# Feed-forward input products of a decoder step: plain blocks replaced by seven products on halves

## The chip, the core and the metric

The kernel runs on one core of one Trainium2 chip. The metric is device time in microseconds for one execution. A core has TensorE (matmuls, with weight loads in a row of their own), VectorE, ScalarE, GpSimd and a queue engine, SyncE, each with an instruction stream of its own, and 16 DMA engines.

## What is computed

One step of a two-layer decoder trunk on 1024 prompt tokens and 8 sample tokens (T = 1032), width 1024: a gated linear recurrence, a feed-forward, a latent attention, a feed-forward. Of the reference, what matters here:

```python
def rmsnorm(x, gain):
    y = xf * lax.rsqrt(jnp.mean(xf * xf, axis=-1, keepdims=True) + EPS)
    return y * gain

def swiglu(h, w_in, w_out):
    g, u = jnp.split(h @ w_in, 2, axis=-1)      # w_in 1024 x 5632
    return (jax.nn.silu(g) * u) @ w_out         # w_out 2816 x 1024

x = x + rmsnorm(mix, g[1])
x = x + rmsnorm(swiglu(rmsnorm(x, g[2]), w_ffn_in[l], w_ffn_out[l]), g[3])
```

## The kernel before, in words

Tokens lie along the free dimension in NS = 3 spans of W = 344 columns; the width lies in KC = 8 chunks of 128 partitions. Every large product is done in three passes: each operand is split into a high and a low fp32r part, and `mm3` (L172) multiplies high by high, high by low and low by high into one PSUM bank (lines L177, L178, L179), each matmul with its own 128 x 128 weight load. `xproduct` (L184) runs `mm3` over the eight chunks of one span: 24 matmuls of 344 columns. `split` (L127) makes a high part on ScalarE (L129) and a low part on VectorE (L130). `weight` (L132) loads 512 KB of weights on SyncE's queue, casts the high part on ScalarE (L151) and subtracts the low part on GpSimd (L155, two pieces of 512).

The four stages follow each other: `hgrn`, `ffn0`, `mla`, `ffn1`. The feed-forward (`ffn`, L533) goes over NF = 22 blocks of 128 hidden columns. For each block and span, `inp` makes g and u by two `xproduct`s, multiplies both by the reciprocal root `r` of the token's mean square (L552, L556 on VectorE: x itself is not normalised), applies silu (L553, ScalarE), multiplies (L557, GpSimd) and splits into `gh`, `gl`. The output products of the block before run between: `out_chunk` for 3 spans x 8 output chunks, 3 matmuls each (72 a block), evacuated by an addition into `acc` on VectorE (L582). The last LAST = 3 blocks are multiplied in `outf` inside the final norm.

`finish` (L296) ends every stage but the last. Per span, `products` makes the eight output chunks and `norm` runs a span behind: reciprocal root of the sum of squares (`rstd`, L192, L198), multiplication into `acc` (L324), residual addition (L325), `put_x` (L213: high and low part of x, L221 and L222, not normalised), squares (L241), and at the end the second root `r`. For the last span that root is left to the feed-forward: the squares are added up into two tiles `ss` (L336), and `r` is made when `inp` first needs it. Four `xproduct`s of the next stage on spans 0 and 1 are run ahead in `finish`.

The engines run in their own order; a tile framework adds the waits and orders the instructions of an engine by program order and due times. Buffers of a pool are reused in turn, which makes a later writer wait for the last reader.

## Time and profile before

| | before |
|---|---|
| median of 3 runs | 2925.95 us (2925.64 to 2926.82) |
| profiled execution | 2927.77 us, its span 2926.0 us |
| TensorE matmul, weight load busy | 2790.2 us (95%), 2623.6 us (90%) |
| VectorE, ScalarE, GpSimd busy | 1718.8 (59%), 1129.5 (39%), 999.3 us (34%) |
| mean DMA rate | 83 GB/s |
| mean granted TensorE clock | 0.977 |

The page comes from one profiled execution. Matmuls are pipelined: their busy times overlap, and the start-to-start time of neighbours tells how fast they go. Weight loads have records of their own (PEld) and overlap the matmuls. A wait is put down to what released it last.

### The profile page before, as it was taken

What the parts mean: (1) busy time and instruction counts of PE and PEld (TensorE: products, weight loads), DVE (VectorE), ACT (ScalarE), POOL (GpSimd) and SP (SyncE); (2) the same over time, 40 slices, a digit from 0 to 9 for tenths busy, and PEclk for the clock granted to TensorE, in tenths of its full rate; (3) what the DMA queues carried; (4) which work ended last, traced back from release to release, by engine and by line L of the source; (5) the groups of instructions that cost most, each with busy time, mean ns of one, the idle gap of its engine ahead of it and who ended that gap; (6) DMA issues with size and microseconds to landing.
All of it is one profiled execution on the core that took longest, in us unless ns stands there. A gap on an engine that the chain in (4) does not pass through costs nothing.

```text
span 2926.0 us, 54566 instructions
## 1 busy us (share of the span) xinstructions
PE 2790.2 (95%) x22360; PEld 2623.6 (90%) x22360; DVE 1718.8 (59%) x3298; ACT 1129.5 (39%) x2422; POOL 999.3 (34%) x912
## 2 busy tenths in 40 slices
PE   7998988889999999999999999979999999999998
PEld 7988888878899999999978899846889999999998
DVE  7888888863444444444358888794363444444435
ACT  7666666655511111111255766523453111111112
POOL 3555555552432233332332111242153332223320
PEclk9999999989999999999999999989999999999999
DMA  5122222152311111111132112486431111111112
GB/s 184 54 67 67 67 67 65 60 191 99 117 48 50 44 44 51 46 49 51 37 100 83 46 48 69 169 346 223 133 107 51 47 48 51 44 44 49 46 61 92
DMA packets 230970, 242.51 MB, mean 83 GB/s; under 512 B 19074, under 2 KB 211120, under 8 KB 224704
## 3 DMA queue, kind: packets, MB, share of 16 engines
q1 hardware_dynamic: 205456, 170.14, 19.0%
q0 software_dynamic: 7456, 43.00, 4.0%
q10 hardware_dynamic: 17808, 25.89, 2.5%
q8 instruction: 176, 2.88, 0.4%
q14 instruction: 74, 0.61, 0.1%
HBM read 194.87 MB, written 44.12 MB: 82 GB/s over the span
## 4 chain that ended last, share of the span: by engine, by line
PE 83%; DVE 9%; ACT 4%; issue 2%; DMA 1%; POOL 1%; SPq 0%; DVEq 0%; ACTq 0%; POOLq 0%
PE ps L177 24%; PE ps L178 24%; PE ps L179 23%; PE ps L252 2%; DVE E L873 1%; DVE turned L1458 1%; PE ps L1385 1%; PE ps L1458 1%; DVE X L877 1%; PE ps L903 1%; PE ps L940 1%; ACT E L875 1%; DVE X L1008 1%; PE ps L198 1%; DVE oy L1010 1%
## 5 line engine op out<-in xcount | busy, mean ns | idle before, releaser
L177 PE MATMUL ps<-xh,w 128*128 128x344 f32 x3360 | 1103.8, 329 | 1.9 <-ACT xh L221 1.9
L178 PE MATMUL ps<-xl,w 128*128 128x344 f32 x3360 | 1083.5, 323 | 1.6 <-DVE xl L222 1.6
L179 PE MATMUL ps<-xh,w 128*128 128x344 f32 x3360 | 1078.7, 322 | 0.0
L155 POOL TENSOR_TENSOR w<-raw,w 128x512 fp32r<-128x512 f32 (+1 forms) x360 | 466.3, 1316 | 809.5 <-ACT w L151 803.0
L177 PEld LDWEIGHTS ps<-xh,w 128*128 128x128 f32 x3360 | 638.6, 190 | 24.7 <-issue 12.1
L178 PEld LDWEIGHTS ps<-xl,w 128*128 128x128 f32 x3360 | 638.5, 190 | 15.3 <-issue 8.3
L179 PEld LDWEIGHTS ps<-xh,w 128*128 128x128 f32 x3360 | 637.5, 190 | 5.7 <-issue 5.6
L582 DVE TENSOR_TENSOR acc<-ps,acc 128x344 f32<-128x344 f32 x864 | 397.4, 513 | 0.0
L151 ACT CAST w<-raw 128x1024 fp32r<-128x1024 f32 (+4 forms) x206 | 206.5, 1004 | 423.7 <-PE ps L179 324.0
L177 PE MATMUL ps<-gh,w 128*128 128x344 f32 x1056 | 338.6, 323 | 0.5 <-ACT gh L129 0.3
L179 PE MATMUL ps<-gh,w 128*128 128x344 f32 x1056 | 338.5, 321 | 0.0
L178 PE MATMUL ps<-gl,w 128*128 128x344 f32 x1056 | 338.0, 320 | 0.0
L557 POOL TENSOR_TENSOR u<-u,a 128x344 f32<-128x344 f32 x132 | 122.1, 926 | 533.6 <-DVE u L556 529.0
L556 DVE TENSOR_TENSOR u<-ps,r 128x344 f32<-128x344 f32 x132 | 68.1, 516 | 388.6 <-PE ps L179 388.4
L129 ACT CAST gh<-u 128x344 fp32r<-128x344 f32 x132 | 63.5, 481 | 504.3 <-POOL u L557 504.3
L552 DVE TENSOR_TENSOR a<-ps,r 128x344 f32<-128x344 f32 x132 | 68.1, 516 | 231.6 <-PE ps L179 225.5
L177 PEld LDWEIGHTS ps<-gh,w 128*128 128x128 f32 x1056 | 198.2, 188 | 5.3 <-issue 1.7
L179 PEld LDWEIGHTS ps<-gh,w 128*128 128x128 f32 x1056 | 198.6, 188 | 1.1 <-issue 1.1
L178 PEld LDWEIGHTS ps<-gl,w 128*128 128x128 f32 x1056 | 198.6, 188 | 1.1 <-DVE gl L130 0.8
L130 DVE TENSOR_TENSOR gl<-u,gh 128x344 fp32r<-128x344 f32 x132 | 70.1, 531 | 150.9 <-ACT gh L129 150.9
L553 ACT ACTIVATE a<-a 128x344 f32<-128x344 f32 x132 | 64.5, 490 | 224.0 <-DVE a L552 223.8
L876 POOL TENSOR_TENSOR X<-lin,E 128x256 f32<-128x256 f32 x112 | 115.8, 1040 | 88.9 <-ACT E L875 32.4
(375 smaller groups left out, 4047.0 us busy)
## 6 DMA issues: line engine op xcount, KB each, us to landing
raw<-in_w_ffn_in_dram SPq DMA_DIRECT2D x88, 512.0 KB
raw<-in_w_ffn_out_dram SPq DMA_DIRECT2D x44, 512.0 KB
raw<-in_w_in_a_dram SPq DMA_DIRECT2D x32, 512.0 KB
xs<-x_d SPq DMA_DIRECT2D x72, 172.0 KB
x_d<-acc ACTq DMA_DIRECT2D x9, 1376.0 KB
x_d<-y SPq DMA_DIRECT2D x3, 1376.0 KB
od_a<-oh ACTq DMA_DIRECT2D x24, 172.0 KB
od_a<-ol ACTq DMA_DIRECT2D x24, 172.0 KB
```

The costliest lines, as they stand in the source:

```text
L130: (lo_eng or self.nc.vector).tensor_tensor(out=lo, in0=src, in1=hi, op=ALU.subtract)
L151: nc.scalar.copy(wh[:, :n], raw[:, :n])
L155: eng.tensor_tensor(out=wl[:, sl], in0=raw[:, sl], in1=wh[:, sl], op=ALU.subtract)
L177: nc.tensor.matmul(out, lhsT=wh, rhs=ah, start=first and i == 0, stop=False)
L178: nc.tensor.matmul(out, lhsT=wh, rhs=al, start=False, stop=False)
L179: nc.tensor.matmul(out, lhsT=wl, rhs=ah, start=False, stop=last and i == n - 1)
L552: nc.vector.tensor_tensor(out=a, in0=pg, in1=r[s], op=ALU.mult)
L553: nc.scalar.activation(out=a, in_=a, func=AF.Silu)
L556: nc.vector.tensor_tensor(out=u, in0=pu, in1=r[s], op=ALU.mult)
L557: nc.gpsimd.tensor_tensor(out=u, in0=u, in1=a, op=ALU.mult)
L582: nc.vector.tensor_tensor(out=acc[s][:, dc, :], in0=po, in1=acc[s][:, dc, :], op=ALU.add)
L876: nc.gpsimd.tensor_tensor(out=Xl[:, :, 0, :], in0=kl[:, :, 0, :], in1=El[:, :, 0, :], op=ALU.mult)
```

## The change

In both feed-forwards:

- The first 4 of the 22 blocks (`PLAIN`) are made as before, two of them partly inside `finish` (`before`). The other 18 are made by seven block products (`PRODUCTS`): the 256 hidden rows of a block (g and u) and the 1024 inputs are halved, and each span's 344 tokens are halved into 2 x 172 (`Q`). Instead of eight products of a weight quarter with an input quarter there are seven, of sums and differences of weight quarters (`make`: S1 to S4, on GpSimd, then split) and of token quarters (`tokens`: T1 to T4, once for a span, then split). `visit` runs the seven for all three spans, each 4 chunks x 3 passes of 172 columns, accumulates some on top of others in PSUM, keeps copies, and forms silu(g) u of both halves.
- For that x is normalised when it is put down: `finish` waits for the second root of every span and then writes high and low part of x r; the multiplications by `r` after the products go.
- The high and low part of silu(g) u go to DRAM (`store`, on ScalarE's queue). The output products follow as a stage of their own; `fetch` brings a block's parts and output weights back on SyncE's queue. Blocks are added up two at a time (`GROUP`), the last three in `outf` as before.

The diff, cut to its core:

```diff
@@ -319 +324 @@ finish: norm
-            xs = pool.tile([P, W], F32, name="xs", tag="xs", bufs=6)
+            xs = pool.tile([P, W], F32, name="xs", tag="xs", bufs=4 if gated else 6)
             nc.sync.dma_start(out=xs, in_=x_d[s][:, c, :])
             nc.vector.scalar_tensor_tensor(out=y, in0=y, scalar=g_post[:, c:c + 1], in1=r1, op0=ALU.mult, op1=ALU.mult)
             (nc.vector if last and c % 3 == 2 else nc.gpsimd).tensor_tensor(out=y, in0=y, in1=xs, op=ALU.add)
-            k.put_x(s, c, y, g_next)
-            if not last:
+            if not gated:
+                k.put_x(s, c, y, g_next)
+            if not last or gated:
                 s2.add(acc[s][:, c:c + 1, :], None, xs)
                 if c == kn['fs']:
                     s2.flush()
@@ -336,10 +342,15 @@
                 (nc.vector if c % 2 else nc.gpsimd).tensor_tensor(out=ss[c % 2], in0=ss[c % 2], in1=xs, op=ALU.add)
             yield
         nc.scalar.dma_start(out=x_d[s], in_=acc[s])
-        if not last:
+        if not last or gated:
             for _ in range(lags[1]):
                 yield
-            rs[s] = yield from s2.rstd(k.new_r(s))
+            r = rs[s] = yield from s2.rstd(k.new_r(s))
+            for c in range(KC if gated else 0):
+                xs = pool.tile([P, W], F32, name="xs", tag="xs", bufs=4)
+                nc.vector.scalar_tensor_tensor(out=xs, in0=acc[s][:, c, :], scalar=g_next[:, c:c + 1], in1=r, op0=ALU.mult, op1=ALU.mult)
+                k.split(k.xh[s][:, c, :], k.xl[s][:, c, :], xs, nc.gpsimd if last and c % 2 else None)
+                yield
...
@@ -358 +369 @@ finish
-    for i, m in enumerate(first):
+    if gated:
+        for _ in gated.before():
+            catch_up(3)
+    for i, m in enumerate(() if gated else first):
...
@@ -524 +538 @@
+LAST, GROUP = 3, 2
+PLAIN, AHEAD = 4, 2
+PRODUCTS = (("A11", "B11"), ("S1", "T1"), ("S2", "T2"), ("S4", "B22"), ("S3", "T3"), ("A12", "B21"), ("A22", "T4"))
+NP_ = len(PRODUCTS)
+KH = KC // 2
+class Gated:
...
+    def store(self, f, s, gs):
+        self.k.nc.scalar.dma_start(out=self.g_d[f, :, :, s * W:(s + 1) * W], in_=gs.bitcast(F32))
+    def plain(self, f, s):
+        k, nc = self.k, self.k.nc
+        wg, wu = self.plain_w[f]
+        pg = k.xproduct(wg, s)
+        a = k.rp.tile([P, W], F32, name="a", tag=f"ss{(f * NS + s) % 2}")
+        nc.scalar.activation(out=a, in_=pg, func=AF.Silu)
+        yield
+        pu = k.xproduct(wu, s)
+        nc.vector.tensor_tensor(out=a, in0=pu, in1=a, op=ALU.mult)
+        gs = self.new_gs()
+        k.split(gs[:, 0], gs[:, 1], a)
+        self.store(f, s, gs)
+        yield
+    def before(self):
+        for f in range(AHEAD):
+            self.plain_weights(f)
+            for s in range(NS - 1):
+                yield from self.plain(f, s)
+    def ahead(self, n):
+        while self.made < n and next(self.making, False) is not False:
+            self.made += 1
...
+    def make(self, f):
+        k, nc = self.k, self.k.nc
+        A = []
+        for i in range(2):
+            raw = k.wp.tile([P, 1024], F32, name="raw", tag="raw", bufs=2)
+            nc.sync.dma_start(out=raw.rearrange("p (a b) -> p a b", a=KC), in_=self.columns(f, i))
+            A += [raw[:, :512], raw[:, 512:]]
+        src = dict(zip(("A11", "A12", "A21", "A22"), A))
+        how = {"S1": ("A21", "A22", ALU.add), "S2": ("S1", "A11", ALU.subtract), "S4": ("A12", "S2", ALU.subtract), "S3": ("A11", "A21", ALU.subtract)}
+        for name, _ in PRODUCTS:
+            if name in how:
+                a, b, op = how[name]
+                src[name] = self.pool.tile([P, 512], F32, name="S", bufs=2)
+                nc.gpsimd.tensor_tensor(out=src[name], in0=src[a], in1=src[b], op=op)
+            w = self.slot()
+            hi, lo = w[:, :512], w[:, 512:1024]
+            k.split(hi, lo, src[name])
+            self.parts[f, name] = [t.rearrange("p (a b) -> p a b", a=KH) for t in (hi, lo)]
+            yield True
+    def tokens(self, s, places):
...
+        t, d = (self.pool.tile([P, KH, Q], F32, name=i) for i in "td")
+        minus = lambda eng, out, a, b: eng.tensor_tensor(out=out, in0=a, in1=b, op=ALU.subtract)
+        plus = lambda out, a, b: nc.vector.tensor_tensor(out=out, in0=a, in1=b, op=ALU.add)
+        for name, a, b in (("T3", B22, B12), ("T1", B12, B11), ("T2", B22, None), ("T4", B21, None)):
+            if b:
+                minus(nc.gpsimd, d, a[1], b[1])
+                minus(nc.vector, t, a[0], b[0])
+                yield
+                plus(t, t, d)
+            else:
+                minus(nc.vector, t, a[0], t)
+                yield
+                plus(t, t, a[1])
+            yield
+            X = self.X[s, name] = places.pop(0)
+            k.split(X[0], X[1], t)
+            yield
+    def visit(self, f):
+        k, nc = self.k, self.k.nc
+        A, C, t1, t2, t5, gs = {}, {}, {}, {}, {}, {}
+        temp = lambda name, s: self.pool.tile([P, Q], F32, name=f"{name}{s}")
+        for name, xname in PRODUCTS:
+            wh, wl = self.parts.pop((f, name))
+            for s in range(NS):
+                xh, xl = self.X[s, xname]
+                if name == "A11":
+                    A[s] = k.psum()[:, :Q]
+                elif name in ("S1", "A12"):
+                    C[s] = k.psum()[:, :Q]
+                to = C[s] if name in ("S1", "S4", "A12") else A[s]
+                more = name not in ("A11", "S1", "A12")
+                k.mm3(to, [((wh[:, j, :], wl[:, j, :]), (xh[:, j, :], xl[:, j, :])) for j in range(KH)], not more, True, more)
+                if name == "A11":
+                    t1[s] = temp("t1", s)
+                    nc.scalar.copy(t1[s], to)
...
+                elif name == "S3":
+                    nc.vector.tensor_tensor(out=t5[s], in0=to, in1=t5[s], op=ALU.add)
+                    nc.vector.tensor_tensor(out=t5[s], in0=t5[s], in1=t2[s], op=ALU.mult)
+                    gs[s] = self.new_gs() if s == 2 else self.pool.tile([P, 2, W], F32R, name="gs", tag="td"[s])
+                    k.split(gs[s][:, 0, Q:], gs[s][:, 1, Q:], t5[s])
...
+                else:
+                    nc.vector.tensor_tensor(out=t1[s], in0=to, in1=t1[s], op=ALU.mult)
+                    k.split(gs[s][:, 0, :Q], gs[s][:, 1, :Q], t1[s])
+                    self.store(f, s, gs[s])
+            yield
+    def run(self, then):
...
+            forming = itertools.chain(*(self.tokens(s, places) for s in range(NS)))
+            plain = [(f, NS - 1) for f in range(AHEAD)] + [(f, s) for f in range(AHEAD, PLAIN) for s in range(NS)]
+            for n, (f, s) in enumerate(plain):
+                self.plain_weights(min(f + (s < NS - 1) if f < AHEAD else f, PLAIN - 1))
+                for _ in self.plain(f, s):
+                    for _ in range(3):
+                        next(forming, None)
+                if s == NS - 2:
+                    self.plain_weights(f + 1)
+                if n == len(plain) - 1:
+                    self.ahead(1)
+            for _ in forming:
+                pass
+            for f in range(PLAIN, NF):
+                for i, _ in enumerate(PRODUCTS):
+                    if i == 0:
+                        steps = self.visit(f)
+                    self.ahead((f - PLAIN) * NP_ + i + 5)
+                    if f == NF - 1 and i == 2:
+                        then()
+                    next(steps)
+def ffn(k, gated, w_out, g_d, end):
     nc, tc = k.nc, k.tc
+    G, wo = {}, {}
+    def fetch(f, new, pool=None):
+        if (f, 0) not in G:
+            t = new([P, 2, T])
+            nc.sync.dma_start(out=t.bitcast(F32), in_=g_d[f])
+            for s in range(NS):
+                G[f, s] = tuple(t[:, i, s * W:(s + 1) * W] for i in range(2))
+        if f not in wo:
+            wo[f] = k.weight(w_out[f * P:(f + 1) * P, :].unsqueeze(1), 1, D, None, pool)
+    def then():
+        fetch(0, lambda shape: k.pre[1].tile(shape, F32R, name="w", tag="w1", bufs=1))
+    gated.run(then)
     with ExitStack() as st:
         accp = st.enter_context(tc.tile_pool(name="accp", bufs=1, reuse_waits="tile"))
+        gp = st.enter_context(tc.tile_pool(name="gp", bufs=2, reuse_waits="tile"))
         acc = [k.new_acc() if k.accs is not None and s < NS - 1 else accp.tile([P, KC, W], F32, name=f"acc{s}") for s in range(NS)]
...
+        f = 0
+        while f < NF - LAST:
+            fs = range(f, min(f + (GROUP if f else 1), NF - LAST))
             for s in range(NS):
+                for dc in range(KC):
+                    n = fs[-1] + 1 + s
+                    if dc == 0 and s < 2 and n < NF:
+                        fetch(n, lambda shape: gp.tile(shape, F32R, name="G", bufs=4), gp if n % 2 else None)
+                    po = out_chunk(k, wo, G, fs, s, dc)
+                    if f == 0:
+                        nc.scalar.copy(acc[s][:, dc, :], po)
+                    else:
+                        nc.vector.tensor_tensor(out=acc[s][:, dc, :], in0=po, in1=acc[s][:, dc, :], op=ALU.add)
+            f = fs[-1] + 1
             k.close_pre()
+        for f in range(NF - LAST, NF):
+            fetch(f, lambda shape: gp.tile(shape, F32R, name="G", bufs=4), gp if f % 2 else None)
```

## Rows read from the trace of the kernel before

**Rows 1.** The page: the chain that ended last, by engine and by line.

```profile
PE 83%; DVE 9%; ACT 4%; issue 2%; DMA 1%; POOL 1%; SPq 0%; DVEq 0%; ACTq 0%; POOLq 0%
PE ps L177 24%; PE ps L178 24%; PE ps L179 23%; PE ps L252 2%; DVE E L873 1%; DVE turned L1458 1%; PE ps L1385 1%; PE ps L1458 1%; DVE X L877 1%; PE ps L903 1%; PE ps L940 1%; ACT E L875 1%; DVE X L1008 1%; PE ps L198 1%; DVE oy L1010 1%
```

**Rows 2.** Busy time by stretch (us, count), granted clock, DMA share, GB/s.

```profile
core 0: us, PE busy (x) PEld busy (x) DVE busy (x) ACT busy (x) POOL busy (x), PEclk, DMA share, GB/s
774.00:1470.00 696.00, 695.70 (x4401) 690.70 (x4401) 301.71 (x636) 141.41 (x229) 219.73 (x189) 1.00 0.16 48
...
2177.00:2870.00 693.00, 692.37 (x4396) 690.75 (x4395) 303.96 (x640) 140.06 (x231) 215.15 (x188) 1.00 0.17 51
```

**Rows 3.** TensorE's timeline (start, duration, line), feed-forward: first and last of 66.

```profile
1199.68 0.32 PE L178 MATMUL ps<-xl,w 128*128 128x344 f32 x1
...
1209.92 0.32 PE L177 MATMUL ps<-gh,w 128*128 128x344 f32 x1
```

**Rows 4.** The same, 256 and 512 columns, early in the attention stage.

```profile
1619.05 0.28 PE L177 MATMUL ps<-w,ch 128*128 128x256 f32 x1
...
1620.12 0.28 PE L177 MATMUL ps<-w,ch 128*128 128x256 f32 x1
...
1608.00 0.40 PE L178 MATMUL ps<-cl,w 128*128 128x512 f32 x1
...
1610.33 0.40 PE L179 MATMUL ps<-ch,w 128*128 128x512 f32 x1
```

**Rows 5.** Weight loads by line and shape: count, busy us, mean ns, idle before.

```profile
L177 PEld LDWEIGHTS ps<-xh,w 128*128 128x128 f32 x3360 | 638.6, 190 | 24.7 <-issue 12.1 <-ACT xh L221 2.2 <-DVE acc L683 1.7
L178 PEld LDWEIGHTS ps<-xl,w 128*128 128x128 f32 x3360 | 638.5, 190 | 15.3 <-issue 8.3 <-DVE xl L222 3.4 <-DVE ss L336 0.2
...
L903 PEld LDWEIGHTS ps<-lin 128*32 128x32 f32 x512 | 6.0, 110 | 1.7 <-issue 1.7
```

**Rows 6.** Loads of L1767: merged in the timeline; then min, median, max ns.

```profile
2039.71 2.42 PEld L1767 LDWEIGHTS ps<-olT,wu 128*128 128x128 f32 x21
...
L1767 PEld LDWEIGHTS ps<-olT,wu x32: 188/192/193, 2039.6 to 2043.1; 128*128 128x128 f32 x32
```

**Rows 7.** VectorE, ScalarE and GpSimd by line and shape (columns as in group 5).

```profile
L582 DVE TENSOR_TENSOR acc<-ps,acc 128x344 f32<-128x344 f32 x864 | 397.4, 513 | 0.0
...
L324 DVE SCALAR_TENSOR_TENSOR acc<-acc,gains,rs_y 128x344 f32<-128x344 f32 x72 | 68.3, 1018 | 0.3
...
L130 DVE TENSOR_TENSOR PTl<-ps,PTh 128x512 fp32r<-128x512 f32 x48 | 32.3, 686 | 1.7 <-ACT PTh L129 1.4
...
L129 ACT CAST PTh<-ps 128x512 fp32r<-128x512 f32 x48 | 27.4, 588 | 29.4 <-PE ps L1385 26.3 <-PE ps L179 2.7
...
L155 POOL TENSOR_TENSOR w<-raw,w 128x512 fp32r<-128x512 f32 x352 | 459.1, 1325 | 724.6 <-ACT w L151 718.0 <-PE ps L981 4.1 <-DVE E L873 2.5
L557 POOL TENSOR_TENSOR u<-u,a 128x344 f32<-128x344 f32 x132 | 122.1, 926 | 533.6 <-DVE u L556 529.0 <-ACT a L553 4.3
```

**Rows 8.** TensorE's timeline at the start of the first feed-forward stage.

```profile
751.83 0.74 PE L198 MATMUL ps<-rs_m,one 128*128 128x344 f32 x2
...
767.30 0.31 PE L179 MATMUL ps<-xh,w 128*128 128x344 f32 x1
774.09 2.63 PE L198 MATMUL ps<-ss,one 128*128 128x344 f32 x4 [6.48 <-DVE a L552]
776.01 0.99 PE L177 MATMUL ps<-xh,w 128*128 128x344 f32 x1
776.81 0.49 PE L178 MATMUL ps<-xl,w 128*128 128x344 f32 x1
...
778.80 0.32 PE L179 MATMUL ps<-xh,w 128*128 128x344 f32 x1
```

**Rows 9.** The stretch with the most DMA (columns as in group 2); a load's landing.

```profile
1890.00:1920.00 30.00, 16.25 (x260) 9.93 (x262) 26.95 (x45) 7.12 (x24) 17.96 (x18) 0.81 0.88 344
...
wu<-in_w_ukv_dram POOLq DMA_DIRECT2D x2, 512.0 KB, 5.8
```

More of the change, by code (lines that the diff above doesn't have):

```diff
@@ L162, in open_pre, with mm3 @@
     def open_pre(self):
-        self.pre, pool = self.right("pre", 2)
-        return pool
+        self.pre = self.right("pre", 2)
+        return self.pre[1]
     def close_pre(self):
         if self.pre is not None:
-            self.pre.close()
+            self.pre[0].close()
             self.pre = None
-    def mm3(self, out, terms, first=True, last=True):
+    def mm3(self, out, terms, first=True, last=True, more=False):
         nc = self.nc
         n = len(terms)
+        skip = {"skip_group_check": True} if more else {}
         for i, ((wh, wl), (ah, al)) in enumerate(terms):
-            nc.tensor.matmul(out, lhsT=wh, rhs=ah, start=first and i == 0, stop=False)
-            nc.tensor.matmul(out, lhsT=wh, rhs=al, start=False, stop=False)
-            nc.tensor.matmul(out, lhsT=wl, rhs=ah, start=False, stop=last and i == n - 1)
+            nc.tensor.matmul(out, lhsT=wh, rhs=ah, start=first and i == 0, stop=False, **skip)
+            nc.tensor.matmul(out, lhsT=wh, rhs=al, start=False, stop=False, **skip)
+            nc.tensor.matmul(out, lhsT=wl, rhs=ah, start=False, stop=last and i == n - 1, **skip)
     def xterm(self, k, s):
@@ L566, in ffn @@
-        units = [inp(f) for f in range(NF)]
-        for f, n in ((0, NS - 1), (1, NS - 1), (0, 1)):
-            for _ in range(n):
-                next(units[f])
-        for f in range(1, NF):
-            if f < NF - 1:
-                for _ in units[f]:
-                    pass
-            k.close_pre()
-            if f <= NF - LAST:
-                for s in range(NS):
-                    for dc in range(KC):
-                        po = out_chunk(k, wo, G, [f - 1], s, dc)
-                        if f == 1:
-                            nc.scalar.copy(acc[s][:, dc, :], po)
-                        else:
-                            nc.vector.tensor_tensor(out=acc[s][:, dc, :], in0=po, in1=acc[s][:, dc, :], op=ALU.add)
+        f = 0
@@ L1793, in tile_yoco_step @@
     pre = {"hgrn": gain(0, 0), "ffn0": gain(0, 2), "mla": None, "ffn1": gain(1, 2)}
-    firsts = {
-        "hgrn": lambda: hgrn_first(a["w_in_a"][0]),
-        "ffn0": lambda: ffn_first(a["w_ffn_in"][0]),
-        "mla": lambda: mla_first(a, cols[:, 64:72]),
-        "ffn1": lambda: ffn_first(a["w_ffn_in"][1]),
-    }
+    firsts = {"hgrn": lambda: hgrn_first(a["w_in_a"][0]), "mla": lambda: mla_first(a, cols[:, 64:72])}
+    g_d = dram.tile([NF, P, 2, T], F32, name="g_d")
+    gated = {f"ffn{l}": Gated(k, a["w_ffn_in"][l], g_d) for l in range(2)}
     k.prefetch(firsts[phases[0]]())
     load = lambda *tiles: load_x(k, a["x_prompt"], a["x_sample"], pre[phases[0]], x_d, *tiles)
-    if phases[0] != "hgrn":
-        with tc.tile_pool(name="ld", bufs=2, reuse_waits="tile") as lp:
-            r = [g() for g in load(lambda: lp.tile([P, D], F32, name="xt"), lambda: lp.tile([P, KC, W], F32, name="y0"), lp)]
     for n, ph in enumerate(phases):
```

89 lines of the change are left out of this document (53 added, 36 removed).

## The prediction

> **What bounds the kernel now.** I read the page's chain of waits first: 83% of what ended last is TensorE, 71% in the three lines of `mm3` [rows 1]. Next I cut the span into stages. In the long stretch of each feed-forward stage (774 to 1470 and 2177 to 2870 us) TensorE is busy without a break at clock 1.00, weight loading is busy for 99%, while VectorE is under half busy, GpSimd under a third, ScalarE a fifth, and the DMA moves about 50 GB/s [rows 2]. So what counts there is the time from the start of one matmul to the start of the next; the busy time of one (0.32 us) overlaps its neighbours and says little.
>
> In the timeline of a feed-forward stretch the first and last of 66 consecutive 344-column matmuls start 10.24 us apart: 10.24 / 65 = 0.157 us each [rows 3]. For 256 columns, 9 intervals take 1.07 us, 0.119 each; for 512, 10 intervals take 2.33 us, 0.233 each [rows 4]. These three lie near one line: (0.233 - 0.119) / 256 = 0.44 ns a column, and 0.119 + 88 x 0.00044 = 0.158 for 344. So at 256 columns and above the moving operand sets the pace. Every one of these matmuls has its own weight load, also where the next one uses the same weights: the lines L177 and L178 share `wh`, and both have 3360 loads [rows 5]. The load must therefore be hidden behind the matmul before it, and at 344 columns it is.
>
> **What the change does to that pace.** A plain block of one span is 2 products x 8 chunks x 3 = 48 matmuls of 344 columns. The new block is 7 products x 4 chunks x 3 = 84 matmuls of 172 columns. Columns fall by an eighth (16512 to 14448), but weight loads rise from 48 to 84 and each has half the columns to hide behind. No matmul of fp32r tiles in the kernel before has fewer than 256 columns, so the price of 172 columns has to be bounded.
>
> From below: the line above, run on to 172, gives 0.119 - 84 x 0.00044 = 0.082 us. From above: it should not be more than the 256-column one, 0.119, at the same clock. Between them stands the load. L1767 has 8-column matmuls, where nothing but loading can take time: 21 loads of 128 x 128 follow each other in 2.42 us, the last taking 0.19, so (2.42 - 0.19) / 20 = 0.1115 us each [rows 6]. Those are fp32 and not fp32r, but the load has the length of an fp32r load (192 against 190 ns), and its length grows with its columns: 110 ns for 32 columns, 192 for 128 [rows 5, 6], 0.85 ns a column, which for 128 columns alone is about 0.107 us. I take 0.1115: it is a stream of the same loads, and it is nearer to 0.119 than to 0.082. Ends for the range: 0.107 and 0.119.
>
> Before I go by that: the 256-column and the 512-column matmuls start 0.119 and 0.233 us apart here [rows 4]. The Trainium skill's page "TensorE: Matmul & The Clock Gate" (section Back-to-back issue gap) gives about 81 ns for a load-and-matmul pair of 128 columns and 131 ns for one of 512. Read between these, 172 columns would cost an estimated 87 ns, and 18 blocks would come out some 24 us shorter instead of 198 us longer. The trace does not agree at 512 columns (233 ns), so I go by the trace and keep the page's case among the rivals.
>
> **The sum, part by part.**
>
> *Seven products for 18 of 22 blocks, 3 spans, 2 layers: 108 block-spans.* Each was 48 x 0.157 = 7.54 us and becomes 84 x 0.1115 = 9.37 us: +1.83 us, +197.6 us in all. With 0.107 it is 84 x 0.107 = 8.99, +157; with 0.119 it is 10.00, +266. Break-even is 7.54 / 84 = 0.0897 us a matmul.
>
> *The other engines in such a block*, 3 x 9.37 = 28 us long. VectorE: seven weight splits of 512 columns at 0.686 us and 3 x 7 operations of 172 columns, each under the 0.513 of 344 columns [rows 7]: at most 4.8 + 10.8 = 15.6 us. ScalarE: seven casts of 512 columns at 0.588 and 3 x 7 shorter operations: at most 16.5 us, plus three stores issued from its queue. GpSimd: four sums of 512 columns at 1.325, 5.3 us [rows 7]. Each store waits on ScalarE's queue for VectorE's low half, some 0.5 us, and the next evacuations stand behind it; a bank has two products (8 us) before it is wanted again. All is hidden, at no cost, and would still be at 0.082 us (20.7 us a block). The weight pieces are made four to five products (16 us) ahead.
>
> *x kept normalised.* Now TensorE stands idle at the start of each feed-forward stage: from 767.30 to 774.09 it waits for VectorE's sums `ss`, and then runs at the lower clock level (1.2 instead of 2.4 GHz), seven intervals in 1.99 us, 0.285 each instead of 0.157, until 778.80 [rows 8]. The work in those 11.5 us would have taken about 2.4: nine matmuls at 0.157, and four with ones that took 1.92 us at half clock, so about 1. About 9 us are lost, and the same wait is in the code of the second layer. After the change the last span first needs its x after eight x-products of the other spans, 8 x 24 x 0.157 = 30 us instead of four, 15 us. Its chain is longer: before, from the last reduction at 751.83 to the use of `ss` at 774.09 it took 22.3 us [rows 8]; eight splits of x drop out of that pass (a ScalarE and a VectorE operation each) and a second reciprocal root (about 4 us) and eight products with splits (about 1 us each on VectorE) follow: 25 to 32 us. That is about the cover. I take a wait of 1 us: net -8 us a layer, -16 in all, between -18 and 0.
>
> *Forming the token sums* (12 tiles a layer of 688 columns) runs beside eight plain block-spans, 60 us. One tile is a chain: GpSimd difference 2 x 0.926 = 1.85 beside VectorE's, then two times 0.513 for the addition, a cast (688/512 of 0.588, 0.79) and again 1.03 for the low part: 4 to 5 us, some 54 us in all [rows 7]. That fits barely; where VectorE and GpSimd hold each other up (L324 takes 1.018 us for as many columns as L582 [rows 7]) it doesn't. +2 us a layer, +4 in all, 0 to +20.
>
> *silu(g) u through DRAM.* The output products keep their number (72 matmuls a block, 11.3 us) and VectorE's additions halve. Every block is now fetched on SP's queue: 1.06 MB and 0.52 MB of weights, 1.58 MB in 11.3 us, 140 GB/s. The trace holds 344 GB/s in one stretch [rows 9], so the middle is covered. Two places are not. At the start, blocks 1 and 2 (3.2 MB) are asked for when block 0's 11.3 us begin: 9.2 us at 344 GB/s, some 2 us to start, and a cast and two GpSimd differences (1.2 + 2.65 [rows 7]) behind the last: about 15 us. +4 us a layer, 0 to 10. At the end, block 21's tile takes the buffer of block 17 (four buffers), which is read until the group before the last three blocks ends; its 1.06 MB take 3 us at 344 GB/s or 11 us at the rate of the one 512 KB load whose landing the profile gives (5.8 us) [rows 9], less the 0.9 us of blocks 19 and 20. +6 us a layer, 2 to 12. Behind that waiting transfer on SP stand only the loads of x for the final norm, wanted a span (some 34 us) later. Together +20 us, 4 to 44.
>
> Sum: 197.6 - 16 + 4 + 20 = +206 us on the profiled execution. Its time is 2927.77 us (a span of 2926.0), 1.8 us above the median of 2925.95, so 3134 there and 3132 for the median. Low end: +157 - 18 + 0 + 4 = +143, 3069. High end: +266 + 0 + 20 + 44 = +330; all four at their worst together is too much, and I stop at 3240.
>
> **Rivals.**
>
> *Loads hide: faster.* If an fp32r load streams faster than the fp32 one of L1767, columns alone count: 0.082 us, 6.89 us a block-span, 0.65 less each, -70 us, and with the +8 of the other parts 2864 us. It decides from any spacing under 0.0897. For it: the load's record of an fp32 transpose or of L1767 is not an fp32r load's pace, and at 344 columns the loads hide wholly. Against it: equal lengths of the loads [rows 5, 6]. Chance 0.09. The figures of the Trainium skill's page "TensorE: Matmul & The Clock Gate", section Back-to-back issue gap, read as above (87 ns), would give an estimated 2910 us.
>
> *Half pace.* If the array falls to the lower of its two clock levels in a stream that is short of columns, or takes two clocks a column below 256, a 172-column matmul takes half of the 0.285 us seen at the lower level [rows 8], 0.1425: 11.97 us a block-span, +478 us, 3412 us. For it: the kernel's own attention never runs fp32r under 256 columns. Against it: the clock stays at 1.00 through all stretches without a wait [rows 2], and here none is expected. Chance 0.06.
>
> *The output stage waits for DRAM.* It decides below 140 GB/s. At 100 GB/s a block takes 15.8 us instead of 11.3: 4.5 x 22 x 2 = +198 on the forecast, 3330 us. Against it 344 GB/s in one stretch [rows 9]. Chance 0.03.
>
> That loads of shared weights are dropped, so that there are fewer than 84, is excluded by the equal counts [rows 5].
>
> **How the numbers follow.** The forecast (loads set the pace) has 0.81, the rivals 0.09, 0.06 and 0.03, and 0.01 is left for a sum that cancels out. The predicted time is the forecast's, 3132; its range 3069 to 3240 leaves 0.19 out. 0.2% (5.9 us) is about what a measurement of this kernel can tell from no change: faster 0.09, same 0.01, slower 0.90.
>
> **What would show it.** In the seven-product stretch, 172-column matmuls starting 0.11 to 0.12 us apart at clock 1.00, weight loading busy all the time, about 28 us a block; 0.082 shows the first rival, 0.14 the second. No idle TensorE over 3 us at the start of each feed-forward; a wait of some us for `G` or `w` at the start of the output products, and one before the last three blocks. The forecast is wrong if the spacing is under 0.09, or if a block's stretch shows TensorE waiting for another engine.

## The result, and the profile after

The changed kernel takes 3178.01 us in the median (3174.66 to 3181.97), the kernel before 2925.8 us (2923.99 to 2926.82) beside it: a ratio of 1.0863 (95%: 1.0844 to 1.0882). That is 252 us longer, where 206 were forecast. The profiled execution has a span of 3180.2 us against 2926.0, 254.2 more, and this is the difference that the traces have to account for.

The page of the changed kernel, its first parts and the groups that answer to [rows 1, 5] (line, engine, operation, tiles and shape, count; then busy us and mean ns of one; then idle time ahead of it and its main releaser):

```profile
span 3180.2 us, 64231 instructions
...
PE 3013.4 (95%) x26276; PEld 2831.5 (89%) x26276; DVE 1908.4 (60%) x3632; ACT 1345.0 (42%) x3168; POOL 918.9 (29%) x794
...
PEclk9999999999999999999999999989999999999999
...
PE 76%; DVE 11%; ACT 5%; issue 3%; DMA 3%; POOL 1%; SPq 0%; ACTq 0%; DVEq 0%; POOLq 0%
...
L180 PE MATMUL ps<-X,w 128*128 128x172 f32 x1440 | 396.0, 275 | 1.9 <-ACT t L675 1.9
...
L180 PEld LDWEIGHTS ps<-X,w 128*128 128x128 f32 x1440 | 276.4, 192 | 2.5 <-ACT t L675 2.2
L182 PEld LDWEIGHTS ps<-X,w 128*128 128x128 f32 x1440 | 276.5, 192 | 0.0
```

Nothing here tells of the loss at first sight: TensorE is busy for 95% of the span, as before, at the same clock. L180 to L182 are now the three lines of `mm3`. What is new are the rows of 128 x 172. Matmuls and loads are still equal in number, so each of the narrow matmuls has its own 128-column load of 192 ns. Where tiles of the token sums are read the operand is called `X`, where parts of x itself are, `xh` or `xl`.

The stretch of the seven products in each feed-forward (columns: stretch, its us, then busy us and count of each engine, granted clock, DMA share, GB/s) answers to [rows 2], and one us of TensorE's timeline in it to [rows 3]:

```profile
847.00:1355.00 508.00, 507.05 (x4539) 506.75 (x4538) 226.79 (x507) 188.84 (x507) 100.48 (x73) 1.00 0.25 77
2384.00:2891.00 507.00, 506.08 (x4531) 505.78 (x4530) 225.34 (x505) 189.08 (x507) 101.39 (x73) 1.00 0.25 80
```

```profile
999.97 0.27 PE L180 MATMUL ps<-X,w 128*128 128x172 f32 x1
1000.08 0.28 PE L181 MATMUL ps<-X,w 128*128 128x172 f32 x1
...
1001.42 0.28 PE L181 MATMUL ps<-xl,w 128*128 128x172 f32 x1
...
1003.99 0.28 PE L180 MATMUL ps<-xh,w 128*128 128x172 f32 x1
```

508.00 / 4538 and 507.00 / 4530 are 0.112 us a matmul at clock 1.00, but for one wait of 0.95 and one of 0.92 us near their starts (the 1.9 us in the first row of 172 columns above); from 999.97 to 1003.99 there are 36 intervals of 0.1117. TensorE and weight loading are both busy for 99.8% of the stretch, the other engines for under half, the DMA moves 77 to 80 GB/s. A matmul of 344 columns took 0.157 [rows 3], so half the columns cost 71% of the time.

The largest stop of TensorE stands at the start of the output products of the first feed-forward. Its timeline, with the idle time ahead and the releaser in brackets, then ScalarE's in the same place:

```profile
1358.71 0.32 PE L182 MATMUL ps<-w 128*128 128x344 f32 x1
1370.00 0.65 PE L180 MATMUL ps<-w 128*128 128x344 f32 x1 [10.97 <-ACT acc L761]
1370.45 0.49 PE L181 MATMUL ps<-w 128*128 128x344 f32 x1
1370.73 0.49 PE L182 MATMUL ps<-w 128*128 128x344 f32 x1
...
1375.59 0.32 PE L181 MATMUL ps<-w 128*128 128x344 f32 x1
1375.75 0.32 PE L182 MATMUL ps<-w 128*128 128x344 f32 x1
```

```profile
1356.42 0.53 ACTq L574 DMA_DIRECT2D g_d<-gs  x1
1368.56 1.04 ACT L152 CAST w<-raw 128x1024 fp32r<-128x1024 f32 x1 [12.53 <-DMA g_d<-gs]
1369.51 1.83 ACT L761 COPY acc<-ps 128x344 f32<-128x344 f32 x5
```

TensorE has filled its PSUM banks with eight output chunks and waits for the first to be copied out (L761). The copies are ScalarE's, and in ScalarE's order they stand behind the cast of block 1's output weights (L152), which waits 12.53 us. Its tile is taken from the pool that is opened where the buffers `gs` lay, so it may be written only when the last store of `gs` has left for DRAM; that store was issued at 1356.42 and shares the DMA engines with four transfers of 1 MB that were asked for from 1353.92 on (from 1357.00 to 1368.50 the DMA is busy throughout, at 405 GB/s). (`wo1`, below, bears this out.) Then TensorE runs at the lower clock until 1375.6, 0.287 us a matmul. From 1358.71 to 1375.59 are 16.88 us for 20 intervals that need 20 x 0.157 = 3.14: 13.7 us lost. In the second layer the same cast waits 5.98 us:

```profile
2905.73 1.04 ACT L152 CAST w<-raw 128x1024 fp32r<-128x1024 f32 x1 [5.98 <-DMA g_d<-gs]
```

```profile
2902.68 0.32 PE L182 MATMUL ps<-w 128*128 128x344 f32 x1
2907.17 0.43 PE L180 MATMUL ps<-G,w 128*128 128x344 f32 x1 [4.17 <-ACT acc L761]
```

There TensorE's stop is 4.49 us from start to start, 4.17 of them idle, and by the same count 6.7 us are lost.

For the trace as a whole I cut it at three instructions whose code is the same in all kernels here: the last matmul of the recurrence, the first transpose of the attention's `cf`, and the first matmul that reads `olT`, behind which the second feed-forward follows. The kernels of the middle columns are told in the next section.

| us | before | after | `plain22` | `evac0` | `wo1` | `pairs` | `pairs_flush` |
|---|---|---|---|---|---|---|---|
| to the recurrence's end | 633.6 | 631.4 | 631.6 | 633.6 | 630.6 | 633.3 | 631.1 |
| first feed-forward | 963.8 | 1090.4 | 971.5 | 1082.0 | 1086.5 | 942.7 | 938.7 |
| attention | 442.3 | 451.6 | 447.2 | 447.6 | 443.1 | 447.0 | 450.7 |
| second feed-forward, output | 886.3 | 1006.8 | 894.2 | 1004.8 | 1003.9 | 871.2 | 865.6 |
| span | 2926.0 | 3180.2 | 2944.5 | 3168.0 | 3164.0 | 2894.2 | 2886.1 |

After minus before is -2.2 + 126.6 + 9.3 + 120.5 = 254.2 us.

### The profile page after: what moved, and what is told of

It reads as the page before. It is cut to its first block, busy times and chain, and to the rows that moved or that the text cites. A ratio compares the mean times of both kernels' runs of the same rounds, so it can differ in the third digit from the quotient of the medians.

```text
span 3180.2 us, 64231 instructions
## 1 busy us (share of the span) xinstructions
PE 3013.4 (95%) x26276; PEld 2831.5 (89%) x26276; DVE 1908.4 (60%) x3632; ACT 1345.0 (42%) x3168; POOL 918.9 (29%) x794
## 4 chain that ended last, share of the span: by engine, by line
PE 76%; DVE 11%; ACT 5%; issue 3%; DMA 3%; POOL 1%; SPq 0%; ACTq 0%; DVEq 0%; POOLq 0%
PE ps L180 22%; PE ps L181 22%; PE ps L182 22%; PE ps L1641 2%; PE ps L255 1%; DVE E L1056 1%; PE ps L1568 1%; DVE X L1060 1%; DMA g_d<-gs 1%; PE ps L1086 1%; PE ps L1123 1%; DVE X L1191 1%; ACT E L1058 1%; ACT w L152 1%; DVE t L640 1%
## 5 line engine op out<-in xcount | busy, mean ns | idle before, releaser
L180 PE MATMUL ps<-xh,w 128*128 128x344 f32 (+1 forms) x2928 | 903.3, 309 | 2.4 <-ACT xh L224 1.6
L181 PE MATMUL ps<-xl,w 128*128 128x344 f32 (+1 forms) x2928 | 886.2, 303 | 1.7 <-DVE xl L225 1.6
L182 PE MATMUL ps<-xh,w 128*128 128x344 f32 (+1 forms) x2928 | 881.9, 302 | 1.6 <-POOL w L156 1.6
L180 PEld LDWEIGHTS ps<-xh,w 128*128 128x128 f32 x2928 | 560.5, 192 | 24.0 <-issue 12.4
L182 PEld LDWEIGHTS ps<-xh,w 128*128 128x128 f32 x2928 | 560.3, 192 | 9.0 <-issue 6.1
L156 POOL TENSOR_TENSOR w<-raw,w 128x512 fp32r<-128x512 f32 (+1 forms) x216 | 288.0, 1354 | 783.1 <-ACT w L152 758.3
L180 PE MATMUL ps<-X,w 128*128 128x172 f32 x1440 | 396.0, 275 | 1.9 <-ACT t L675 1.9
L181 PE MATMUL ps<-X,w 128*128 128x172 f32 x1440 | 395.0, 274 | 0.0
L182 PE MATMUL ps<-X,w 128*128 128x172 f32 x1440 | 394.9, 274 | 0.0
L763 DVE TENSOR_TENSOR acc<-ps,acc 128x344 f32<-128x344 f32 x432 | 222.7, 517 | 225.6 <-PE ps L182 224.8
L180 PE MATMUL ps<-G,w 128*128 128x344 f32 x1008 | 326.0, 323 | 6.9 <-ACT acc L761 4.2
L181 PE MATMUL ps<-G,w 128*128 128x344 f32 x1008 | 324.7, 322 | 0.0
L182 PE MATMUL ps<-G,w 128*128 128x344 f32 x1008 | 323.8, 321 | 0.5 <-POOL w L156 0.5
L152 ACT CAST w<-raw 128x1024 fp32r<-128x1024 f32 (+4 forms) x134 | 130.2, 975 | 432.6 <-PE ps L182 253.6
L625 POOL TENSOR_TENSOR S<-raw 128x512 f32<-128x512 f32 x72 | 98.6, 1369 | 719.4 <-DMA raw<-in_w_ffn_in_dram 618.6
L180 PEld LDWEIGHTS ps<-X,w 128*128 128x128 f32 x1440 | 276.4, 192 | 2.5 <-ACT t L675 2.2
L182 PEld LDWEIGHTS ps<-X,w 128*128 128x128 f32 x1440 | 276.5, 192 | 0.0
L181 PEld LDWEIGHTS ps<-X,w 128*128 128x128 f32 x1440 | 276.5, 192 | 0.0
L180 PEld LDWEIGHTS ps<-G,w 128*128 128x128 f32 x1008 | 190.7, 189 | 12.0 <-issue 5.7
L182 PEld LDWEIGHTS ps<-G,w 128*128 128x128 f32 x1008 | 190.8, 189 | 1.9 <-issue 1.1
```

The costliest lines, as they stand in the source:

```text
L152: nc.scalar.copy(wh[:, :n], raw[:, :n])
L156: eng.tensor_tensor(out=wl[:, sl], in0=raw[:, sl], in1=wh[:, sl], op=ALU.subtract)
L180: nc.tensor.matmul(out, lhsT=wh, rhs=ah, start=first and i == 0, stop=False, **skip)
L181: nc.tensor.matmul(out, lhsT=wh, rhs=al, start=False, stop=False, **skip)
L182: nc.tensor.matmul(out, lhsT=wl, rhs=ah, start=False, stop=last and i == n - 1, **skip)
L625: nc.gpsimd.tensor_tensor(out=src[name], in0=src[a], in1=src[b], op=op)
```

## The experiments

The theory: an fp32r matmul cannot start faster than its weight load, 0.112 us for 128 columns, so below some 240 moved columns the load and not the columns sets the pace. Rivals: the pace has another reason (a fixed price of an instruction; columns that pass more slowly in short matmuls; the DMA of the changed kernel), or the loss is not in the pace but in what was built around it (x kept normalised, the way through DRAM).

**What a load costs: `series`.** The kernel before, with nine series of 64 fp32r matmuls behind its last output; their sums go nowhere.

```diff
+    for m, n in ((P, W), (P, 256), (P, W // 2), (P, W // 4), (P, 32), (64, W // 2), (64, W // 4), (32, W // 2), (P, W // 2)):
+        pp = k.psum()
+        for i in range(64):
+            nc.tensor.matmul(pp[:m, :n], lhsT=w[:, i % 2, i % 8 * P:i % 8 * P + m], rhs=x[:, i % 2, :n], start=i == 0, stop=i == 63)
```

> The kernel before, with nine series of 64 fp32r matmuls after its last output, each series with one width of the loaded weights and one number of moved columns; their sums go nowhere. If the load sets the pace of short matmuls: 0.157 us from start to start for 128 x 344 (weights x columns), 0.119 for 128 x 256, and 0.112 for 128 x 172, 128 x 86 and 128 x 32 alike; with half the weights, 64 x 172 falls to the line of the columns, 0.082, and 64 x 86 to about 0.058; 32 x 172 stays at 0.082. If a fixed price of one matmul sets it, 64 x 172 and 32 x 172 stay at 0.112. If short fp32r matmuls move slower than a column a clock, 86 and 32 columns are well under 0.112 with full weights.

Each row of this view lies inside one series: in order 128 weight columns by 344, 256, 172, 86 (two rows), 32 moved columns, 64 by 172 (two rows), 64 by 86, 32 by 172, and 128 by 172 again. Columns: stretch, us, busy us and count of the matmuls, the same of the loads, clock, DMA.

```profile
2913.00:2922.00 9.00, 9.00 (x59) 9.00 (x58) 1.00 0.43 158
2923.00:2930.00 7.00, 7.00 (x61) 7.00 (x60) 1.00 0.00 0
2931.00:2937.00 6.00, 6.00 (x56) 6.00 (x55) 1.00 0.01 3
2938.00:2941.50 3.50, 3.50 (x33) 3.50 (x33) 1.00 0.00 0
2942.00:2946.00 4.00, 4.00 (x21) 4.00 (x20) 0.50 0.00 0
2948.00:2960.00 12.00, 12.00 (x58) 12.00 (x58) 0.50 0.01 1
2961.00:2965.00 4.00, 4.00 (x30) 4.00 (x29) 0.50 0.00 0
2966.00:2967.50 1.50, 1.50 (x22) 1.50 (x20) 1.00 0.00 0
2968.00:2971.00 3.00, 3.00 (x55) 3.00 (x54) 1.00 0.00 0
2972.00:2976.00 4.00, 4.00 (x53) 4.00 (x51) 1.00 0.00 0
2977.00:2983.00 6.00, 6.00 (x57) 6.00 (x55) 1.00 0.00 0
```

The start-to-start times, from the starts themselves, are 0.158 us for 344 columns, 0.120 for 256, 0.112 for 172 (both times), and 0.112 still for 86: with full loads nothing goes below 0.112 at the upper clock. With loads of 64 columns, 86 moved columns take 0.058, about half; so it is not a fixed price of an instruction. With loads of 64 and of 32 columns, 172 moved columns take 0.080 both times (the former once the clock is up): there the moved columns set the pace, and 172 of them would have taken 0.08, as the line through 256 and 512 columns had it. The pace is the longer of the two, load and columns. It has nothing to do with the changed kernel's DMA, since here there is hardly any. The fall of the clock in the 86-column series had not been expected; it is told at the end.

**The pace alone: `halves`.** The kernel before, with each product on x in the feed-forward made on two halves of 172 columns: the same columns, twice the loads, nothing else of the change.

```diff
+        if halves:
+            for c in (slice(0, W // 2), slice(W // 2, W)):
+                self.mm3(pp[:, c], [((wt[0][:, j, :], wt[1][:, j, :]), tuple(x[:, c] for x in self.xterm(j, s))) for j in range(KC)])
+            return pp
```

> The kernel before, with every input product of the feed-forward made on two halves of 172 columns, same sums, no seven products: 256 products (264 less the eight made ahead) of 48 matmuls in place of 24. If the load sets the pace: 48 x 0.112 - 24 x 0.157 = +1.61 us each, +411 us, 3337 us. If the columns do: 48 x 0.082 - 3.77 = +0.17 each, +43 us, 2969 us. If the after kernel's pace of 0.112 comes from its sums, copies or banks and not from the loads, this one is near 2969 too.

It took 3322.99 us, 1.1355 of the kernel before (1.1332 to 1.1378): 396 us for splitting alone. In its first feed-forward:

```profile
800.00:1650.00 850.00, 849.68 (x7013) 846.87 (x7012) 296.23 (x615) 122.62 (x200) 207.64 (x175) 1.00 0.12 37
```

850 / 7012 = 0.1212 us a matmul. A block and span there has 96 of 172 columns and 24 of 344 for the output: (96 x 0.112 + 24 x 0.157) / 120 = 0.121. So it is the number of loads, without sums, without DRAM, and at clock 1.00.

**What was built around it: `plain22`.** The changed kernel with all 22 blocks plain, and no token sums: x kept normalised and the way through DRAM stay.

```diff
-PLAIN, AHEAD = 4, 2
+PLAIN, AHEAD = NF, 2
-            forming = itertools.chain(*(self.tokens(s, places) for s in range(NS)))
+            forming = iter(())
```

> The changed kernel with all 22 blocks plain: x normalised, silu(g) u through DRAM, blocks added up two at a time, but no seven products and no token sums. If the seven products cost 108 x (84 x 0.112 - 48 x 0.157) = 202 us of the 252 and the rearrangement the other 50: 2976 us. If the 50 belong to the seven products (token sums, weight pieces, what follows them): within 10 us of 2926.

2950.84 us, a ratio of 1.0087 (1.007 to 1.0104): 24 us over the kernel before beside it. So neither expected case held: half of the 50 us belongs to what was built around the products. The other 227 us of the change come with the seven products. 108 block-spans of 84 x 0.112 - 48 x 0.157 = 1.87 us are 202 of them; the stop at the start of the output products, which this kernel does not have, is most of the rest (13.7 + 6.7 = 20.4). Its profiled execution is one of the shorter, 18.5 us over before by the table: 7.7 in the first feed-forward, 7.9 in the second, 4.9 in the attention, 2.0 less ahead of them.

**Seven products without the narrow tiles: `pairs`.** If loads set the price, the same saving of products should win as soon as the halves are wide enough. Here the two halves of the tokens are spans 0 and 1, 344 columns each; the seven products serve these two, and span 2 is made plain from the same weight parts: 84 + 48 = 132 matmuls of 344 columns a block instead of 144.

```diff
-PRODUCTS = (("A11", "B11"), ("S1", "T1"), ("S2", "T2"), ("S4", "B22"), ("S3", "T3"), ("A12", "B21"), ("A22", "T4"))
+PRODUCTS = (("A11", "B11"), ("S1", "T1"), ("S2", "T2"), ("S4", "B22"), ("S3", "T3"), ("A12", "B21"), ("A21", None), ("A22", "T4"))
...
+            if name in ("A11", "A21"):
+                L = k.psum()[:, :W]
+                k.mm3(L, terms(w, self.last[0]), True, False)
+            elif name in ("A12", "A22"):
+                k.mm3(L, terms(w, self.last[1]), False, True)
```

> The changed kernel with the seven products on spans 0 and 1 as the two halves, 344 columns each, and span 2 plain: a block has 7 x 12 + 48 = 132 matmuls of 344 columns in place of 3 x 84 of 172. If the pace is set by loads up to about 240 columns and by columns above: 132 x 0.157 = 20.7 us a block against 28.2, and against 22.6 of plain blocks: 36 x 1.9 = 68 us under the all-plain version, near 2908 us. If the seven products are held up by their sums, copies or weight pieces: not below the all-plain version, and TensorE waits in the stretch.

2894.8 us, 0.9887 (0.9871 to 0.9904): faster than the kernel before by 32 us, and 56 under `plain22`, where 12 x 0.157 x 18 x 2 = 68 were worked out. In its middle:

```profile
860.00:1080.00 220.00, 220.00 (x1402) 220.00 (x1402) 129.32 (x184) 89.61 (x182) 62.60 (x44) 1.00 0.31 100
```

220 / 1402 = 0.157: the pace of full columns. So where the load stays hidden the seven products save most of what they should, 56 of 68 us (which waits take the other 12 was not settled), and at 172 columns the same products cost 227.

**The stop at the start of the output products: `wo1`, `evac0`.** Two ways at the changed kernel. First, block 1's output weights from the pool of ordinary weights, which does not lie where `gs` lay:

```diff
-fetch(n, lambda shape: gp.tile(shape, F32R, name="G", bufs=4), gp if n % 2 else None)
+fetch(n, lambda shape: gp.tile(shape, F32R, name="G", bufs=4), gp if n % 2 and n > 1 else None)
```

> The changed kernel with the output weights of block 1 in the other weight pool. In the changed kernel TensorE stands still for 11.3 us after the first 8 output chunks of the first feed-forward (1358.7 to 1370.0) and runs at the lower clock for 5 us more; in the second it is 4.5 us. If the cause is ScalarE's cast of block 1's weights, whose buffer lies where the last parts of silu(g) u still wait for their store, with the PSUM copies queued behind it: the cast no longer waits and 13 to 19 us go, about 3161 us. If TensorE waits for parts of blocks 1 and 2 coming back from DRAM: the stop moves from chunk 8 to chunk 24 and stays nearly as long, 3172 us or more.

3169.06 us, 1.0832 (1.0813 to 1.085), about 9 us less, but the stop only fell from 11.29 to 9.27 us (from start to start), so neither side had it right. ScalarE's and GpSimd's timelines show what came in its place:

```profile
1353.95 1.05 ACT L152 CAST w<-raw 128x1024 fp32r<-128x1024 f32 x1
...
1355.01 1.85 ACT L761 COPY acc<-ps 128x344 f32<-128x344 f32 x5
1366.66 1.04 ACT L152 CAST w<-raw 128x1024 fp32r<-128x1024 f32 x1 [9.81 <-DMA g_d<-gs]
1367.62 3.93 ACT L761 COPY acc<-ps 128x344 f32<-128x344 f32 x11
```

```profile
1367.84 2.51 POOL L156 TENSOR_TENSOR w<-raw,w 128x512 fp32r<-128x512 f32 x2 [10.22 <-DMA raw<-in_w_ffn_out_dram]
```

The first cast no longer waits; the next one does, 9.81 us, now for its weights. Its row still names the store, but GpSimd, which needs the same `raw`, waits in the same stretch for the weights' transfer, and that was asked for at 1357.65, behind the four of `G`. Five copies pass between the two casts, and the others stand behind the second. Second, then, the copies on VectorE, whatever the casts wait for:

```diff
-                        nc.scalar.copy(acc[s][:, dc, :], po)
+                        nc.vector.tensor_copy(acc[s][:, dc, :], po)
```

> The changed kernel with the PSUM copies of the first output block on VectorE instead of ScalarE, nothing else. With the other weight pool the stop at the start of the output products only fell from 11.3 to 9.3 us: ScalarE's next cast then waited for weights that had come late behind the parts of blocks 1 and 2. If the stop is made by casts standing in front of PSUM copies on ScalarE, whatever the cast waits for: it goes, and at most the wait for block 1 or 2 after chunk 24 is left (0 to 6 us): 8 to 15 us less, 3163 to 3170 us. If TensorE lacks data: the stop stays at 9 to 11 us, 3178 us.

3168.34 us, 1.0814 (1.0792 to 1.0836). TensorE no longer stops behind eight chunks, only once all 24 of block 0 are made, and there for the weights of block 1 themselves:

```profile
1369.97 0.66 PE L180 MATMUL ps<-G,w 128*128 128x344 f32 x1 [3.00 <-ACT w L152]
```

10.97 us of idle time became 3.00, which shows the order on ScalarE's queue to be the cause of the difference in the first layer. In the second layer, where the stop had come behind all 24 chunks already, it stays (4.29 us idle against 4.17) and now ends with the cast itself: that part is the late weights, not the copies behind them. In `wo1`, where these weights don't wait for the store, 2.62 us of it are left, until parts arrive from DRAM:

```profile
2891.89 0.63 PE L180 MATMUL ps<-G,w 128*128 128x344 f32 x1 [2.62 <-DMA G<-g_d]
```

**The wait in the norm: `pairs_x6`, `pairs_x6_p3`, `pairs_flush`.** In the changed kernel the squares of a span keep TensorE waiting inside `finish` (waits of TensorE between 625 and 850 us; total, times, longest):

```profile
PE ps L255 <- ACT xs L244: 3.0, 1, 3.0
PE ps L201 <- ACT rs_m L263: 1.6, 2, 1.1
PE ps L182 <- POOL w L156: 0.8, 2, 0.5
```

I first held the four buffers of `xs` (six before) to be the reason, and gave `pairs` six, with the space taken from `gs`; then also one plain block fewer.

```diff
-            xs = pool.tile([P, W], F32, name="xs", tag="xs", bufs=4 if gated else 6)
+            xs = pool.tile([P, W], F32, name="xs", tag="xs", bufs=6)
-        return self.k.pre[1].tile([P, 2, W], F32R, name="gs", tag="gs", bufs=2)
+            return self.k.pre[1].tile([P, 2, W], F32R, name="gs", tag="gs", bufs=1)
```

> The pair version with six buffers instead of four for x of the last layer's norm (the room comes from one buffer less for the parts of silu(g) u in the norm; the blocks after it take theirs from another pool). In the pair version, as in the changed kernel, TensorE waits 3.0 us in the first norm and 5.7 us in the second for squares that wait for a transfer of x into one of the four buffers. If the four buffers are the cause: these waits go, 5 to 10 us, about 2887 us. If the chain of the norm itself is too long: no change, 2895 us.

```diff
-PLAIN, AHEAD = 4, 2
+PLAIN, AHEAD = 3, 2
```

> The same with 3 plain blocks in place of 4, one more block by seven products: 1.9 us less a layer, 4 us in all, if the token sums still end within five plain block-spans (38 us); if they don't, TensorE waits before the first seven-product block and nothing is gained.

2897.13 us (0.9904, 0.9886 to 0.9922) and 2895.34 us (0.989, 0.9872 to 0.9909): no gain over `pairs` in either. In `pairs_x6` the wait of the first layer stayed, and another grew:

```profile
PE ps L201 <- ACT rs_m L263: 6.9, 2, 6.1
PE ps L255 <- ACT xs L244: 3.0, 1, 3.0
```

So in the first layer the number of buffers was not the cause. In the second (2020 to 2220 us) the waits for squares fell from the first to the second of these rows, so there it had a part:

```profile
PE ps L255 <- ACT xs L244: 5.7, 3, 2.5
PE ps L255 <- ACT xs L244: 3.0, 1, 3.0
```

In the code the sums of squares of a span are started after half of its squares (`s2.flush` when `c == kn['fs']`), and TensorE, which takes its work in order, stands before the next ones until ScalarE has made them. `pairs_flush` starts them when all eight squares are there; it also has the copies of block 0 on VectorE.

```diff
-                if c == kn['fs']:
+                if c == kn['fs'] and not gated:
                     s2.flush()
```

> The pair version with the sums of squares of x started only when all eight squares are made, and the PSUM copies of the first output block on VectorE. In the pair version TensorE waits in the two norms 3.0 and 5.7 us for squares of which it was given the sum too early. If the early sum is the cause: these waits go, up to 8 us, about 2887 us. If the chain of the norm is: TensorE waits as long at the second sum, 2895 us.

2884.36 us, 0.9848 (0.9832 to 0.9864), the fastest of all here, 10 us under `pairs` and 43 under the kernel before. The wait at 672 us is gone, but in the norm of the last span one of 4.0 us has come in its place:

```profile
766.11 1.78 PE L255 MATMUL ps<-xs,one 128*32 128x344 f32 x4 [3.97 <-ACT xs L244]
```

In all, the waits for squares are not shorter than in `pairs`: 4.4 us where it had 3.0 in the first layer, 7.8 where it had 5.7 in the second.

```profile
PE ps L255 <- ACT xs L244: 4.4, 2, 4.0
PE ps L255 <- ACT xs L244: 7.8, 4, 4.3
```

So it is not the early sum alone that makes TensorE wait: by these rows the other case held, in which it waits as long for the later sums, and the 10 us don't come from shorter waits for squares. The run has two edits in it, and the share of each is not shown. The kernel before starts its sums as early, and its TensorE doesn't wait for a square between 625 and 850 us. What the change also did was to take the steps of the norm faster between the output chunks, three at a time instead of two:

```diff
-            catch_up(kn['rate'] if i else kn['rate0'])
+            catch_up(3 if gated else kn['rate'] if i else kn['rate0'])
```

That puts the sums earlier among the products in the program's order. Whether it makes the wait, no run tested.

## Why the prediction was right, and where it was off

**The pace.** 0.112 us against the 0.1115 that was taken; +202 us against 197.6. The low end of the range rests on a slip: 0.85 ns a column is 0.109 us for 128 columns, not 0.107, and 84 such matmuls cost some +175 us instead of +157; the forecast itself does not use it. The step that chose between 0.082 and 0.119 by the fp32 loads of [rows 6] held: an fp32r load of the same length keeps the same pace, which `series` shows by itself. The rival by columns alone (2864 us) fell with it; its 0.082 is real (0.080), but only with loads of 64 or 32 columns. The Trainium skill's page "TensorE: Matmul & The Clock Gate", section LDWEIGHTS (loading the stationary operand), puts a load at its columns divided by 1.2, in ns, an estimated 107 ns for 128. The trace agrees within 5% at clock 1.00 (112 ns) and not at 0.50, where a load took 213. The estimate of 87 ns from that page's section Back-to-back issue gap did not hold.

**Half pace.** Over two stretches of 507 us the clock was 1.00, so this rival fell for 172 columns. It was no empty one: at 86 columns, in `series`, the clock did fall.

**The other engines.** Hidden, as forecast: VectorE is busy for 45% of the stretch, ScalarE 37%, GpSimd 20%, and TensorE waits once in each, 0.95 and 0.92 us, for a copy of a product.

**x kept normalised.** Forecast -8 us a layer, and this step had the wrong sign; its range, -18 to 0 in all, does not hold the +17 either. The idle time of [rows 8] did go, as it should. But the step counted only the end of the chain, the last span, and put every other wait at nothing. Where it failed is its cover: the eight x-products do hide the last root, but TensorE now waits for the squares of another span, whose sums stood in its order before without a wait. It stops at 672.12, and from 676.00 to 679.00 the granted clock is 0.50:

```profile
672.12 0.31 PE L182 MATMUL ps<-xh,w 128*128 128x344 f32 x1
675.42 1.00 PE L255 MATMUL ps<-xs,one 128*32 128x344 f32 x2 [3.00 <-ACT xs L244]
```

And the last span's squares, which VectorE and GpSimd had summed into `ss`, are now 16 more matmuls of L255. If every interval from the end of the recurrence to 800 us is set against the clean one of its shape, 30.6 us are lost there, and 21.1 were before: +9.5 instead of -8. The second layer gives 28.3 against 20.5, +7.8. Together +17 for -16: most of what the forecast lacked. No run changed this part alone; the figure is read from the two traces, and the levels depend on what is taken as clean, the differences hardly. `plain22`, with x normalised and without the long stop, points the same way: its two feed-forwards are 7.7 and 7.9 us longer than before. What makes the wait at 672.12 is left open (see `pairs_flush`).

**Token sums.** Forecast +2 us a layer; the transition at 847 us shows no wait. They fit beside the plain blocks.

**silu(g) u through DRAM.** Forecast +4 a layer at the start of the output products; 13.7 and 6.7 were lost. The transfers were late by about the 15 us that were worked out, and block 0's 11.3 us of work should have covered most of it. That the 15 us came out is in part luck: 3.2 MB were counted at 344 GB/s, and 5.82 MB moved between 1349 and 1371 us, at 405 GB/s in the middle of it. The step that failed is this cover: after eight chunks TensorE had no free PSUM bank, because the copies that free them stood behind a waiting cast in ScalarE's order. The prediction asked what stands behind a waiting store on ScalarE, and did not ask it of a waiting cast. The Trainium skill's page "TensorE: Matmul & The Clock Gate", section "Architectural detail: the array is 16× 32×32, not 1× 128×128", says that ScalarE's and VectorE's queues are strictly first in, first out. The trace agrees: five copies start at 1369.51, right behind the cast that began at 1368.56. Before the last three blocks 6 us a layer were forecast; the first layer shows no stop, the second one of 2.96 us at 3115.17, with the lower clock behind it.

**The attention.** Its code is the same, and the forecast had nothing for it. It took 442.3 us before and 451.6 after, and between 443.1 and 450.7 in the other kernels of the table, in no order that goes with their edits. +9.3 us of the profiled difference lie there; the start of the program gives 2.2 back. About half of the 9.3 is idle time of TensorE for which the profile shows no releaser, 6.3 us before (first row) and 11.1 after:

```profile
PE ps L1458 <- issue: 6.3, 4, 3.2
PE ps L1641 <- issue: 11.1, 6, 4.7
```

The mean granted clock there fell from 0.97 to 0.96. Why is left open.

**The sum.** 202 + 17 + 20.4 + about 4 before the last three blocks + 9.3 - 2.2 is about 251 of the profiled 254.2 us. The sign and the main term were right for the reason given; of the 46 us that the forecast lacks in the median some 44 are the norm (33, from -16 to +17), the start of the output products (12), the attention and the start of the program (7) and the pace (4), less what the token sums (4) and the last blocks (8) did not cost.

## What to carry over

Count weight loads beside columns: here a matmul of fp32r tiles costs the longer of 0.112 us and its columns (0.080 for 172, 0.120 for 256, 0.157 for 344), so a scheme that saves an eighth of the products pays only on tiles that hide the load, as `pairs` did with the same seven products at 344 columns (-32 us, and -43 with `pairs_flush`). When a transfer is put in front of a stage, look at what stands behind each instruction that waits for it: a cast that waits on the engine that also empties PSUM stops TensorE after as many chunks as there are free banks. When a wait is taken away from the end of a chain, look for the same wait at its other turns: here starting the sums later only moved it to the last span.

## What the hardware showed that was not expected

A load follows the clock: the 128-column load took 0.112 us at clock 1.00, and 0.213 at 0.50 in the series of 32 moved columns, where only loading can set the pace.

In the same run the clock fell without any pause of TensorE. The 172-column series ran at 1.00 from 2930.2 us on; the 86-column series followed at 2937.3, at the same 0.112 us a matmul, busy throughout, and at 2941.65 the granted clock went from 1.00 to 0.50. It stayed there through the rest of that series and that of 32 columns, and came back at 2965.55, in the series of 64 weight columns by 172. The 172-column streams of the changed kernel, at the same 0.112, kept 1.00 for 507 us. What it is in the 86-column stream that the chip answers to, these rows don't show, and one run of one series is all there is.
